# A decoder trunk on one core: the last LayerNorm's reciprocal root rewritten with one step on GpSimd, and the 16 spatial products of the gMLP mixer dealt out differently

## Chip, core and metric

The kernel is one program on one core of a Trainium2 chip. The metric is the device time of one execution in microseconds (us). Engines are named as in the profile: PE (TensorE, matmuls; PEld is its weight load), DVE (VectorE), ACT (ScalarE), POOL (GpSimd), SP (SyncE, which here only starts DMAs).

## What is computed

Two post-norm layers over x (1 x 1024 x 1024). Layer 0 mixes tokens with a gated MLP (gMLP), layer 1 with dilated attention; each mixer is followed by a squared-ReLU MLP. After each of the four sub-layers the residual is normalized. Cut to what the change touches:

```python
def layer_norm(x, g, b):
    mu = jnp.mean(xf, axis=-1, keepdims=True)
    var = jnp.mean(jnp.square(xf - mu), axis=-1, keepdims=True)
    y = (xf - mu) * lax.rsqrt(var + LN_EPS) * g + b

def mixer_a(h, w_in, b_in, vn_g, vn_b, w_s, b_s, w_out):
    u, v = jnp.split(jax.nn.gelu(h @ w_in + b_in), 2, axis=-1)
    v = layer_norm(v, vn_g, vn_b).reshape(B, S // CHUNK, CHUNK, A_GROUPS, A_GROUP_DIM)
    z = jnp.einsum('gts,bnsgc->bntgc', w_causal, v) + b_s.T[:, :, None]
    return (u * z.reshape(B, S, A_WIDTH)) @ w_out

for i in range(DEPTH):                      # DEPTH = 2
    x = layer_norm(ALPHA * x + gate * mixer(h), ln_g[i, 0], ln_b[i, 0])
    x = layer_norm(ALPHA * x + gate * squared_relu_mlp(h), ln_g[i, 1], ln_b[i, 1])
```

## The kernel before

The program runs five stages one after another: the gMLP mixer (to about 306 us), the first MLP, the attention, its output product, and the second MLP, whose end is the end of the program. Every product is done in three passes of 128x512 matmuls on pairs (hi, lo) of rounded numbers; making the pair from a raw tile takes a cast (usually on ACT, L107) and a subtraction (usually on DVE, L108), the helper `split`. Instructions are recorded in the order of the code; the Tile layer then orders each engine's queue, and each engine runs its queue in order.

**The mixer.** v stands in the tile `vz` (8 row blocks of 128 tokens by 1024 columns), in two halves of 512 columns. `norm_v(ch, i)` normalizes half `ch` of row block `i`: one ACT step (L583) and two DVE steps (L584, L585). `spatial(g)` does the product of group g, 64 columns of all eight row blocks: the pair `vhi`, `vlo` (two buffers each, so group g+2 takes over those of group g), three matmuls into the bank `psz` (L377), and on ACT the result back into `vz` (L595). Groups 0 to 7 read the first half of the columns, groups 8 to 15 the second, so `norm_v(1, ...)` of all eight row blocks must be done before group 8. `u_unit(u)` makes 128 columns of u (48 matmuls into `psu`), `gate_unit(u)` transposes groups 2u and 2u+1 (`pszt`, L615) and multiplies them with u (L616). A loop over u deals the groups out between the units:

```python
for u in range(KD):
    for _ in range((2, 2, 2, 3, 3, 4, 0, 0)[u]):
        g = groups_of.popleft()
        spatial(g)
        if g < NT:
            norm_v(1, g)
```

Meanwhile a background queue (`tick`) works through the adaLN products: it loads `adaw` tiles, adds them up on DVE in `adaacc` (L133), and sums over partitions with the small matmuls `psa` (L167, L168; L159 and L160 for a gate). The output weights `wout` and the last `winu` tiles are loaded and split in the same stretch.

**The second MLP's end.** Its down product goes through seven passes of eight steps, each with its own pair of splits, prepared two steps ahead (`rhi`, `lhi` on ACT, `rlo`, `llo` on DVE, L972 on PE). The last three steps are done row block by row block for m = 0 to 3, 18 matmuls each, and each row block then ends so: add the product to the residual (L992), statistics (L256), mean and variance (L321 into `mv`), `rstd_of` (L244 variance plus epsilon; L245 square root on ACT; L246 reciprocal r; L248 r*r*(var+eps); L252 times -0.5 plus 1.5; L253 times r), then the result in two steps over 1024 columns (L341: (z - mean) * g; L342: times rstd, plus b) and the DMA out. The row of g (`lng`) is loaded by `affine`, in the middle of the down product. Row blocks 4 to 7 end earlier, between other steps.

Of the kernel before, what the change touches and what calls it, by code (L numbers as in the profile page):

```python
# [10 lines left out]
F32 = mybir.dt.float32  # L11
F32R = mybir.dt.float32r
AF = mybir.ActivationFunctionType
ALU = mybir.AluOpType
# [3 lines left out]
P = 128  # L18
S = 1024
D = 1024  # L20
NT = S // P
# [8 lines left out]
EPS = 1e-5  # L30
# [5 lines left out]
def trunk(ctx: ExitStack, tc: tile.TileContext, x, c, ada_w, ada_b, ln_g, ln_b, a_w_in, a_b_in,  # L36
# [4 lines left out]
    V, A, G, T = nc.vector, nc.scalar, nc.gpsimd, nc.tensor  # L41

    def pool(stack, name, bufs, **kw):
        return stack.enter_context(tc.tile_pool(name=name, bufs=bufs, reuse_waits="tile", **kw))

    cst = pool(ctx, "cst", 1)
    small = pool(ctx, "small", 4)
# [10 lines left out]
    ident = cst.tile([P, P], F32, name="ident")  # L58
    make_identity(nc, ident[:])
    ones_r = cst.tile([P, P], F32R, name="ones_r")  # L60

    n_ln = 4 * KD
    o_g, o_b, o_s, o_i = 0, n_ln, 2 * n_ln, 2 * n_ln + 16
# [177 lines left out]
    def rstd_of(dst, var, n, name):  # L241

        t = small.tile([P, 3, n], F32, name=name, tag=f"rstd{n}", bufs=4 if n == 1 else 1)
        V.tensor_scalar(t[:, 0, :], var, EPS, None, ALU.add)  # L244
        A.activation(t[:, 1, :], t[:, 0, :], AF.Sqrt)  # L245
        V.reciprocal(t[:, 2, :], t[:, 1, :])  # L246
        if n == 1:
            V.scalar_tensor_tensor(t[:, 1, :], t[:, 2, :], t[:, 2, :], t[:, 0, :], ALU.mult, ALU.mult)  # L248
        else:
            V.tensor_tensor(t[:, 1, :], t[:, 2, :], t[:, 2, :], op=ALU.mult)  # L250
            V.tensor_tensor(t[:, 1, :], t[:, 1, :], t[:, 0, :], op=ALU.mult)
        V.tensor_scalar(t[:, 1, :], t[:, 1, :], -0.5, 1.5, ALU.mult, ALU.add)  # L252
        V.tensor_tensor(dst, t[:, 1, :], t[:, 2, :], op=ALU.mult)  # L253
# [9 lines left out]
    def row_tile(src, name, tag):  # L263
        t = vec.tile([P, D], F32, name=name, tag=tag)
        nc.sync.dma_start(t[:], src.partition_broadcast(P))
        return t
# [3 lines left out]
    class Residual:  # L270
# [19 lines left out]
        def affine(self, j):  # L290
            i, s = divmod(j, 2)
            self.g = row_tile(ln_g[i, s], f"lng_{j}", "lng")
            self.b = row_tile(ln_b[i, s], f"lnb_{j}", "lnb")

        def add_x(self, i):
            j = self.j
            t = work.tile([P, D], F32, name=f"res_{j}_{i}", tag="res", bufs=3)
            nc.sync.dma_start(t[:], (spill[j - 1] if j else x_in)[i * P : (i + 1) * P, :])
            V.scalar_tensor_tensor(self.acc[i][:], t[:], ALPHA, self.acc[i][:], ALU.mult, ALU.add)
# [18 lines left out]
        def moments(self, i):  # L318

            mv = self.mv[i] = small.tile([P, 4], F32, name=f"mv_{self.j}_{i}", tag="mv")  # L320
            V.bn_aggr(mv[:, 0:2], self.st.pop(i)[:])  # L321
            rstd_of(mv[:, 2:3], mv[:, 1:2], 1, f"r_{self.j}_{i}")

        def finish(self, i, halves=(0, 1)):
            j = self.j
# [132 lines left out]
    def mixer_a():  # L458
        nonlocal ada_p, vec
        with ExitStack() as ph:  # L460
# [88 lines left out]
            with tc.tile_pool(name="mixA1", bufs=3, reuse_waits="tile") as a1:  # L549
# [22 lines left out]
                mv = ap.tile([P, 4, NT], F32, name="mv_v")  # L572
# [7 lines left out]
                def norm_v(ch, i):  # L580
                    w = slice(ch * HALF, (ch + 1) * HALF)
                    z = vz[:, i, w]
                    A.activation(z, z, AF.Identity, bias=mv[:, 3, i : i + 1], scale=mv[:, 2, i : i + 1])  # L583
                    V.tensor_tensor(z, z, vg[:, w], op=ALU.mult)  # L584
                    V.tensor_tensor(z, z, vb[:, w], op=ALU.add)  # L585

                def spatial(g):
                    w = slice(g * HEAD, (g + 1) * HEAD)
                    hi = a1.tile([P, NT, HEAD], F32R, name=f"vhi_{g}", tag="vhi", bufs=2)
                    lo = a1.tile([P, NT, HEAD], F32R, name=f"vlo_{g}", tag="vlo", bufs=2)  # L590
                    split(hi[:], lo[:], vz[:, :, w])
                    p = bank("mm", f"psz_{g}")
                    p3 = p[:].rearrange("p (n c) -> p n c", c=HEAD)
                    passes(p3, [([t[:, g, :] for t in wsT], [hi[:], lo[:]])])
                    A.activation(vz[:, :, w], p3, AF.Identity, bias=cols[:, o_s + g : o_s + g + 1])  # L595
# [26 lines left out]
                uts = [u_unit(0), u_unit(1)]  # L622
                groups_of = deque(range(16))
                for u in range(KD):
                    for _ in range((2, 2, 2, 3, 3, 4, 0, 0)[u]):
                        g = groups_of.popleft()
                        spatial(g)
                        if g < NT:
                            norm_v(1, g)
                    if u + 2 < KD:  # L630
                        uts.append(u_unit(u + 2))
                    gate_unit(u, uts[u])
# [1209 lines left out]
    with ExitStack() as ph:  # L1842
        open_psum(ph, "A", tr=3, mm=5)
        done = mixer_a()
# [33 lines left out]
```

## Time and profile before

| | us |
|---|---|
| three runs | 2695.23, 2697.97 (median), 2700.25 |
| the profiled execution's own time | 2695.87 |
| its span, first to last instruction | 2694.1 |
| PE busy in the span | 2650.0 |
| DVE busy in the span | 1992.2 |
| ACT busy in the span | 1375.9 |
| POOL busy in the span | 116.5 |

The span is 1.8 us shorter than the execution's own time; the predicted times are times of the execution. A row of the timeline gives the start (us from the first instruction), the length, the engine, the line, the operation and its tiles, and in brackets how long the engine had been idle before and what released it. A row of the waits gives the total, the number and the longest. Matmuls are pipelined: the next one starts about 0.23 us after the last, though each is listed with 0.39 us.

### The profile page before, as it was taken

To read this page: it belongs to the slowest core of one execution; us is meant where nothing else is said; L and a number is where in the kernel's file an instruction comes from. 1 tells how busy PE (TensorE), PEld (TensorE's weight loads), DVE (VectorE), ACT (ScalarE), POOL (GpSimd) and SP (SyncE) were. 2 spreads that over 40 slices of the span, in tenths; PEclk is the share of its full clock that TensorE was granted. 3 is DMA by queue.
4 is the path that set the end of the run, shared out by engine and by line. 5 is a ranking of instruction groups with operands and counts; after the bars stand their busy time and mean duration, and the time that the engine had idled before them with its cause. 6 is when DMAs were issued, how large, how long until landed. Compare 5 with 4: busy or idle time off the path is not lost.

```text
span 2694.1 us, 37100 instructions
## 1 busy us (share of the span) xinstructions
PE 2650.0 (98%) x13242; PEld 2190.0 (81%) x13242; DVE 1992.2 (74%) x3610; ACT 1375.9 (51%) x2601; POOL 116.5 (4%) x193
## 2 busy tenths in 40 slices
PE   6999999999999999999999999999999999999998
PEld 5787878888888888888888888888888788888887
DVE  6687698787888788655647777777658966577877
ACT  3354375555544464333436666666655655553332
POOL 1000000000000001111111000000010000000000
PEclk9999999999999999999999999999999999999999
DMA  8444337676967745655476545555683664485562
GB/s 266 149 129 130 125 122 230 221 240 232 360 225 251 243 157 192 208 182 191 165 224 176 138 127 139 140 145 145 206 233 122 200 206 154 148 308 196 179 209 82
DMA packets 340781, 504.77 MB, mean 187 GB/s; under 512 B 51900, under 2 KB 177252, under 8 KB 340596
## 3 DMA queue, kind: packets, MB, share of 16 engines
q1 hardware_dynamic: 324212, 443.68, 51.9%
q0 software_dynamic: 16384, 58.73, 6.0%
q8 instruction: 104, 1.70, 0.3%
q14 instruction: 81, 0.66, 0.1%
HBM read 365.40 MB, written 136.92 MB: 186 GB/s over the span
## 4 chain that ended last, share of the span: by engine, by line
PE 56%; issue 22%; DVE 9%; DMA 8%; POOL 2%; ACT 2%; SPq 0%; POOLq 0%; DVEq 0%; ACTq 0%
PE psd L972 11%; PE psua L810 8%; PE psk L1402 6%; PE psq L1402 6%; DMA adaw<-in_ada_w_dram 4%; PE psuc L810 4%; PE psd_wout L398 3%; PE pv L1571 3%; PE sc L1491 3%; PE psu L377 2%; PE psub L810 2%; PE psv L480 2%; DVE adaacc L133 1%; PE pT L1544 1%; POOL v L1278 1%
## 5 line engine op out<-in xcount | busy, mean ns | idle before, releaser
L810 PE MATMUL psua<-right,left 128*128 128x512 f32 x1536 | 364.8, 391 | 0.5 <-ACT part L815 0.2
L972 PE MATMUL psd<-rhi,lhi 128*128 128x512 f32 x896 | 349.7, 390 | 0.0
L972 PE MATMUL psd<-rlo,lhi 128*128 128x512 f32 x896 | 348.8, 389 | 0.0
L972 PE MATMUL psd<-rhi,llo 128*128 128x512 f32 x896 | 348.6, 389 | 0.0
L810 PEld LDWEIGHTS psua<-right,left 128*128 128x128 f32 x1536 | 286.4, 188 | 63.8 <-ACT part L815 1.6
L1513 ACT ACTIVATE p<-p,stat 128x128 f32<-128x128 f32 (+1 forms) x384 | 168.8, 441 | 98.1 <-DVE stat L1511 97.9
L972 PEld LDWEIGHTS psd<-rhi,lhi 128*128 128x128 f32 x896 | 168.2, 188 | 35.8 <-ACT part L841 0.9
L972 PEld LDWEIGHTS psd<-rhi,llo 128*128 128x128 f32 x896 | 168.3, 188 | 35.1
L972 PEld LDWEIGHTS psd<-rlo,lhi 128*128 128x128 f32 x896 | 168.3, 188 | 34.4
L810 PE MATMUL psuc<-right,left 128*128 128x512 f32 x768 | 188.6, 392 | 0.1
L133 DVE SCALAR_TENSOR_TENSOR adaacc<-adaw,silu_c,adaacc 128x512 f32<-128x512 f32 x168 | 128.5, 775 | 59.4 <-DMA adaw<-in_ada_w_dram 58.5
L810 PEld LDWEIGHTS psuc<-right,left 128*128 128x128 f32 x768 | 143.0, 188 | 31.9 <-DVE right L108 1.2
L108 DVE TENSOR_TENSOR pTlo<-pT,pThi 128x512 fp32r<-128x512 f32 (+1 forms) x160 | 99.3, 621 | 75.6 <-ACT pThi L107 74.6
L107 ACT CAST left<-ws 128x512 fp32r<-128x512 f32 x128 | 79.4, 621 | 140.5 <-DVE ws L730 103.6
L108 DVE TENSOR_TENSOR llo<-lraw,lhi 128x1024 fp32r<-128x1024 f32 x112 | 136.3, 1218 | 2.3 <-ACT lhi L107 2.3
L108 DVE TENSOR_TENSOR left<-ws,left 128x512 fp32r<-128x512 f32 x128 | 88.0, 689 | 66.2 <-ACT left L107 63.9
L1402 PE MATMUL psk<-form_L,wqk_hi 128*128 128x512 f32 x384 | 127.1, 412 | 0.2 <-DVE qlo L108 0.2
L1402 PE MATMUL psq<-form_L,wqk_hi 128*128 128x512 f32 x384 | 126.4, 410 | 0.0
L107 ACT CAST lhi<-lraw 128x1024 fp32r<-128x1024 f32 x112 | 117.1, 1047 | 7.1 <-PE psd L972 3.3
L1301 PE MATMUL psv<-vrhi,form_S 128*128 128x512 f32 x384 | 119.9, 390 | 0.8 <-ACT vrhi L107 0.5
L1511 DVE CUSTOM_DVE_ANT_0 p<-sc,bias 128x128 f32<-128x128 f32 (+1 forms) x384 | 113.9, 346 | 5.6 <-PE sc L1491 4.6
L107 ACT CAST pThi<-pT 128x512 fp32r<-128x512 f32 (+1 forms) x160 | 84.7, 530 | 59.3 <-PE pT L1544 42.6
(332 smaller groups left out, 6070.9 us busy)
## 6 DMA issues: line engine op xcount, KB each, us to landing
lraw<-forms SPq DMA_DIRECT2D x112, 512.0 KB, 3.6
adaw<-in_ada_w_dram SPq DMA_DIRECT2D x192, 256.0 KB, 3.0
up<-in_mlp_w_up_dram SPq DMA_DIRECT2D x64, 512.0 KB, 4.4
forms<-s SPq DMA_DIRECT2D x128, 256.0 KB, 3.0
rraw<-in_mlp_w_down_dram SPq DMA_DIRECT2D x64, 512.0 KB, 5.4
forms<-part SPq DMA_DIRECT2D x96, 256.0 KB, 2.4
v<-vs POOLq DMA_DIRECT2D x48, 512.0 KB, 3.7
vraw<-in_b_w_qkv_dram SPq DMA_DIRECT2D x42, 512.0 KB, 3.9
```

The source lines that it names most:

```text
L107: first = A.copy(hi, src) if hi_engine is A else hi_engine.tensor_copy(hi, src)
L108: return first, lo_engine.tensor_tensor(lo, src, hi, op=ALU.subtract)
L133: ins = V.scalar_tensor_tensor(acc[:], raw[:], silu_c[:, k : k + 1], acc[:], ALU.mult, ALU.add)
L398: T.matmul(p[:], stat[a][:, k, o : o + P], u[b][:, w], start=n == 0, stop=n == count - 1)
L810: T.matmul(acc, w[:, a, k, :], right[p][:, b, k, :], start=p in (1, 2, 5) and k + a + b == 0, stop=k == 3 and a == 1, skip_group_check=True)
L972: ins = T.matmul(sums[kind, m][:], l[a][:, k, m * P : (m + 1) * P], r[b][:, k, :], start=p in (1, 5, 2, 3) and kp + k + a + b == 0, stop=k ...
L1301: T.matmul(acc, rows[:, m * P : (m + 1) * P], cols_, start=p in (1, 2, 5) and kp + k + a + b == 0, stop=kp == 1 and k == 1 and a == 1, ski ...
L1402: T.matmul(p[:], wu[a][:, k * P : (k + 1) * P], h_op(k, half, b), start=k + c_ == 0, stop=k == KD - 1 and c_ == 2)
L1491: T.matmul(banks[e][:, sl], q_[a][rows, tq], k_[b][rows, keys], start=c_ == 0, stop=c_ == 2)
L1511: V.tensor_tensor_reduce(out=pr, in0=banks[e][:, sl], in1=st["bias"][:, width - w :], scale=-0.125, scalar=3e38, op0=ALU.add, op1=ALU.min, ...
L1513: A.activation(pr, pr, AF.Exp, bias=nm, scale=-1.0, accum_out=l)
L1571: T.matmul(pvs[b][:, q0 % HALF : q0 % HALF + w_], stt, x_[:, o_ : o_ + w_], start=not begun[b], stop=left[b] == 0, skip_group_check=True)
```

## The change

Three edits, in four places.

1. In the last LayerNorm alone (j = 3) the correction of the root goes from three DVE steps to two. With s = r*r*(var+eps), r*(1.5 - 0.5*s) is -0.5 * (s - 3) * r; the kernel now leaves rstd without the -0.5, and the row of g is multiplied by -0.5 once, on ACT, behind its load. Variance plus epsilon for s is made on GpSimd instead of DVE, beside the square root, which adds epsilon itself from a new constant tile `eps`.
2. That constant is set by DVE at the start of the program. The tile lies ahead of nearly all others: in the built program 3068 SBUF tiles lie 32 bytes further, 343 lie where they lay.
3. The groups are dealt out as 2, 2, 3, 3, 3, 3 instead of 2, 2, 2, 3, 3, 4, and `norm_v(1, ...)` of the eight row blocks is spread over groups 0 to 5 instead of 0 to 7.

```diff
+    eps = cst.tile([P, 1], F32, name="eps")
+    V.memset(eps[:], EPS)
...
             self.b = row_tile(ln_b[i, s], f"lnb_{j}", "lnb")
+            if j == 3:
+                A.mul(self.g[:], self.g[:], -0.5)
...
             V.bn_aggr(mv[:, 0:2], self.st.pop(i)[:])
-            rstd_of(mv[:, 2:3], mv[:, 1:2], 1, f"r_{self.j}_{i}")
+            if self.j < 3:
+                rstd_of(mv[:, 2:3], mv[:, 1:2], 1, f"r_{self.j}_{i}")
+                return
+            t = small.tile([P, 3, 1], F32, name=f"r_{self.j}_{i}", tag="rstd1", bufs=4)
+            G.tensor_scalar(t[:, 0, :], mv[:, 1:2], EPS, None, ALU.add)
+            A.activation(t[:, 1, :], mv[:, 1:2], AF.Sqrt, bias=eps[:])
+            V.reciprocal(t[:, 2, :], t[:, 1, :])
+            V.scalar_tensor_tensor(t[:, 1, :], t[:, 2, :], t[:, 2, :], t[:, 0, :], ALU.mult, ALU.mult)
+            V.scalar_tensor_tensor(mv[:, 2:3], t[:, 1, :], -3.0, t[:, 2, :], ALU.add, ALU.mult)
...
-                    for _ in range((2, 2, 2, 3, 3, 4, 0, 0)[u]):
+                    for _ in range((2, 2, 3, 3, 3, 3, 0, 0)[u]):
                         g = groups_of.popleft()
                         spatial(g)
-                        if g < NT:
-                            norm_v(1, g)
+                        for i in ((0, 1), (2,), (3,), (4,), (5, 6), (7,))[g] if g < 6 else ():
+                            norm_v(1, i)
```

In the changed file the lines stand 2 lower from the constant on, 4 lower behind `affine` and 12 lower behind `moments`. Where the change moves rows, on three engines:

PE, in the mixer, where group 8 is multiplied (names as in the text above; the first number in a name is the group or the unit). Before:

```order
L377 MATMUL psz_7_1819<-vhi_7_1815,wsT_0_777 128x512
L377 MATMUL psz_7_1819<-vlo_7_1816,wsT_0_777 128x512
L377 MATMUL psz_7_1819<-vhi_7_1815,wsT_1_778 128x512
L167 MATMUL psa_1_0_1_1912<-ones_r_78,adahi_1_0_1_1898 128x2
L377 MATMUL psz_8_1831<-vhi_8_1827,wsT_0_777 128x512
L377 MATMUL psu_5_0_1843<-hT_0_0_0_129,winu_5_hi_1838 128x512
L377 MATMUL psu_5_0_1843<-hT_0_0_1_130,winu_5_hi_1838 128x512
L377 MATMUL psu_5_0_1843<-hT_0_0_0_129,winu_5_lo_1839 128x512
L377 MATMUL psz_8_1831<-vlo_8_1828,wsT_0_777 128x512
```

In the change group 8 stands second behind group 7, and the third of its cluster, group 9, comes behind eight `psa` and five transposes; these are the last rows of that stretch:

```order
L170 MATMUL psa_1_0_1_1923<-ones_r_78,adalo_1_0_1_1910 128x2
L627 MATMUL pszt_3_0_1942<-ident_73,vz_129 128x128 x4
L627 MATMUL pszt_3_1_1948<-ident_73,vz_129 128x128
L389 MATMUL psz_9_1842<-vhi_9_1838,wsT_0_779 128x512
L389 MATMUL psu_5_0_1854<-hT_0_0_0_131,winu_5_hi_1849 128x512
L389 MATMUL psu_5_0_1854<-hT_0_0_1_132,winu_5_hi_1849 128x512
L389 MATMUL psu_5_0_1854<-hT_0_0_0_131,winu_5_lo_1850 128x512
L389 MATMUL psu_5_0_1854<-hT_0_0_0_131,winu_5_hi_1849 128x512
L389 MATMUL psz_9_1842<-vlo_9_1839,wsT_0_779 128x512
```

So the third group of a cluster has more other work ahead of it than before. PE at the last groups, 14 and 15 before:

```order
L159 MATMUL psa_1_2_0_2165<-adahi_1_2_0_2043,ones_r_78 128x512
L160 MATMUL psa_1_2_0_2165<-adalo_1_2_0_2044,ones_r_78 128x512
L615 MATMUL pszt_5_0_2183<-ident_73,vz_127 128x128 x4
L615 MATMUL pszt_5_1_2189<-ident_73,vz_127 128x128 x4
L377 MATMUL psz_14_2086<-vhi_14_2082,wsT_0_777 128x512
L377 MATMUL psz_15_2095<-vhi_15_2091,wsT_0_777 128x512
L377 MATMUL psu_7_0_2107<-hT_0_0_0_129,winu_7_hi_2102 128x512
L377 MATMUL psz_14_2086<-vlo_14_2083,wsT_0_777 128x512
```

and now, with group 14 done in one piece and 15 transposes ahead of group 15:

```order
L389 MATMUL psz_14_2088<-vhi_14_2084,wsT_0_779 128x512
L389 MATMUL psz_14_2088<-vlo_14_2085,wsT_0_779 128x512
L389 MATMUL psz_14_2088<-vhi_14_2084,wsT_1_780 128x512
L627 MATMUL pszt_5_0_2185<-ident_73,vz_129 128x128 x4
L627 MATMUL pszt_5_1_2191<-ident_73,vz_129 128x128 x4
L627 MATMUL pszt_6_0_2197<-ident_73,vz_129 128x128 x4
L627 MATMUL pszt_6_1_2203<-ident_73,vz_129 128x128 x3
L389 MATMUL psz_15_2097<-vhi_15_2093,wsT_0_779 128x512
L389 MATMUL psu_7_0_2109<-hT_0_0_0_131,winu_7_hi_2104 128x512
```

The transposes of unit 6 used to stand behind the whole of `psu_7`; most of them now stand ahead of group 15. DVE at the end of the program, from the last row block's statistics on (`mv_3`, `r_3` and `xo` 24702 are the last row block's, `mv_2` and `xo` 24669 the one's before it), before:

```order
L256 BN_STATS st_3_24572<-acc_3_22393 128x6
L252 TENSOR_SCALAR r_2_24662<-r_2_24662 128x1
L321 BN_AGGR mv_3_24693<-st_3_24572 128x2
L253 TENSOR_TENSOR mv_2_24660<-r_2_24662 128x1
L244 TENSOR_SCALAR r_3_24695<-mv_3_24693 128x1
L341 SCALAR_TENSOR_TENSOR xo_24702<-acc_3_22393,mv_3_24693,lng_23717 128x512
L342 SCALAR_TENSOR_TENSOR xo_24669<-xo_24669,mv_2_24660,lnb_23719 128x1024
L246 RECIPROCAL r_3_24695<-r_3_24695 128x1
L341 SCALAR_TENSOR_TENSOR xo_24702<-acc_3_22393,mv_3_24693,lng_23717 128x512
L248 SCALAR_TENSOR_TENSOR r_3_24695<-r_3_24695 128x1
L252 TENSOR_SCALAR r_3_24695<-r_3_24695 128x1
L253 TENSOR_TENSOR mv_3_24693<-r_3_24695 128x1
```

and now:

```order
L334 SCALAR_TENSOR_TENSOR mv_2_24657<-r_2_24659 128x1
L258 BN_STATS st_3_24571<-acc_3_22395 128x6
L354 SCALAR_TENSOR_TENSOR xo_24665<-xo_24665,mv_2_24657,lnb_23721 128x1024
L325 BN_AGGR mv_3_24689<-st_3_24571 128x2
L353 SCALAR_TENSOR_TENSOR xo_24697<-acc_3_22395,mv_3_24689,lng_23719 128x512
L332 RECIPROCAL r_3_24691<-r_3_24691 128x1
L353 SCALAR_TENSOR_TENSOR xo_24697<-acc_3_22395,mv_3_24689,lng_23719 128x512
L333 SCALAR_TENSOR_TENSOR r_3_24691<-r_3_24691 128x1
L334 SCALAR_TENSOR_TENSOR mv_3_24689<-r_3_24691 128x1
```

Two small rows of each row block are gone, and the second result step of the row block before stands ahead of the last one's L325 instead of behind its first L353. On ACT, in the middle of the second MLP's down product (pass 6 is the third), the scaling of g stands between two casts:

```order
L109 CAST lhi_5_7_22971<-lraw_5_7_22931 128x1024
L109 CAST rhi_5_7_22976<-heldt_1_22412 128x1024
L109 CAST lhi_6_0_23010<-lraw_6_0_22968 128x1024
L297 ACTIVATE lng_23719<-lng_23719 128x1024
L109 CAST rhi_6_0_23015<-heldt_0_22411 128x1024
```

Before, the two casts of step 6_0 stood one behind the other.

## The prediction

> **What bounds the kernel now.** I read the page's first part, then the waits of PE, then the timeline at the places that the change touches.
>
> ```profile
> span 2694.1 us, 37100 instructions
> PE 2650.0 (98%) x13242; PEld 2190.0 (81%) x13242; DVE 1992.2 (74%) x3610; ACT 1375.9 (51%) x2601; POOL 116.5 (4%) x193
> ```
>
> PE idles 44.1 us of 2694.1, so work that lies beside PE is worth nothing by itself; an edit pays where PE waits or after PE's last matmul.
>
> ```profile
> PE psa L167 <- ACT adahi L107: 16.8, 3, 13.9
> ...
> PE psz L377 <- DVE vlo L108: 0.7, 1, 0.7
> PE psz L377 <- ACT vhi L107: 0.7, 1, 0.7
> ```
>
> Of the waits that the list names, the mixer's spatial products hold only 1.4 us. The longest, 13.9, is at the start, where the first adaLN sum is formed. The end is DVE's: PE's last matmul starts at 2683.81, and DVE works in one piece from row block 0 to the last result step.
>
> ```profile
> 2683.58 0.39 PE L972 MATMUL psd<-rlo,lhi 128*128 128x512 f32 x1
> 2683.81 0.39 PE L972 MATMUL psd<-rhi,llo 128*128 128x512 f32 x1
> ```
>
> **Part 1, the groups.** The timeline of the first wait, PE and ACT:
>
> ```profile
> 210.81 0.16 PE L167 MATMUL psa<-ones_r,adahi 128*128 128x2 f32 x1
> ...
> 211.62 1.09 PE L615 MATMUL pszt<-ident,vz 128*128 128x128 f32 x8
> 212.47 0.47 PE L377 MATMUL psz<-vhi,wsT 128*128 128x512 f32 x1
> ...
> 213.01 0.63 PE L377 MATMUL psz<-vhi,wsT 128*128 128x512 f32 x2
> ...
> 213.71 0.39 PE L377 MATMUL psz<-vhi,wsT 128*128 128x512 f32 x1
> ...
> 214.75 0.50 PE L377 MATMUL psz<-vhi,wsT 128*128 128x512 f32 x1 [0.65 <-ACT vhi L107]
> ...
> 247.25 0.50 PE L377 MATMUL psz<-vlo,wsT 128*128 128x512 f32 x1 [0.69 <-DVE vlo L108]
> ```
>
> ```profile
> 213.50 0.69 ACT L595 ACTIVATE vz<-psz,cols 128x512 f32<-128x512 f32 x1 [0.58 <-PE psz L377]
> 214.09 0.61 ACT L107 CAST vhi<-vz 128x512 fp32r<-128x512 f32 x1
> ```
>
> Group 8 is third behind 6 and 7 and takes over group 6's `vhi`. Group 6's last matmul starts at 213.01, ACT writes its result back from 213.50, casts until 214.70, and PE starts group 8 at 214.75: 1.74 us that PE must fill between the first product's last matmul and the third product. Before, it had that matmul's own step, group 7 (together 0.93, to 213.94) and one `psa`, and stood 0.65.
>
> In the new order every cluster but the first two has three groups, with this ahead of the third. Eight `psa` take 0.81 (210.81 to 211.62), eight transposes 0.85 (211.62 to 212.47). Group 6: 0.93 plus eight `psa`, 1.74: just covered. Group 9: 0.93 plus 0.81 plus five transposes (0.53), 2.27. Group 12: 0.93 plus eight transposes (0.85) plus two `psa` of 512 columns at about 0.23, 2.24. Group 15: 0.93 plus 15 transposes (1.6), 2.5. All reach 1.74, so both waits should go: 1.34 us. New ones are possible. Fifteen transposes for units 5 and 6 need banks that DVE must empty, and DVE may be in a 128x1024 subtraction for `wout` (such a step takes 1.22 us by L1722's row in part 2); and the `vlo` behind a `vhi` has just three `psu` matmuls (0.7) to hide its 0.69. I charge 0.35 for both, nearer to the single waits shown than to the 1.22. Term: **-1.0 us**, between -1.3 and +0.9 (both waits kept in a new place, plus 0.9).
>
> What moves with it: the second half's norms come up to three groups earlier, two DVE steps and one ACT step each. They pass background additions and `winu` splits, all needed a unit later (48 matmuls 0.23 us apart, 11 us), and DVE's longest waits between 150 and 330 us are for its loads:
>
> ```profile
> DVE adaacc L133 <- DMA adaw<-in_ada_w_dram: 11.4, 13, 2.0
> ```
>
> The DMAs of `winu_7`, `wout_0`, `wout_2` and `wout_3` move by one to three places on SP, far ahead of use. I price these at nothing; without that cover a late weight would cost PE a whole split, 1 to 2 us.
>
> **Part 2, the last rows.** DVE at row block 0:
>
> ```profile
> 2673.45 0.21 DVE L321 BATCH_NORM_AGGREGATE mv<-st 128x2 f32<-128x12 f32 x1
> 2673.69 0.15 DVE L244 TENSOR_SCALAR r<-mv 128x1 f32<-128x1 f32 x1
> 2673.76 1.27 DVE L341 SCALAR_TENSOR_TENSOR xo<-acc,mv,lng 128x1024 f32<-128x1024 f32 x1
> 2674.95 0.15 DVE L246 RECIPROCAL r<-r 128x1 f32<-128x1 f32 x1
> 2675.14 0.22 DVE L248 SCALAR_TENSOR_TENSOR r<-r 128x1 f32<-128x1 f32 x1
> 2675.40 0.15 DVE L252 TENSOR_SCALAR r<-r 128x1 f32<-128x1 f32 x1
> 2675.59 0.16 DVE L253 TENSOR_TENSOR mv<-r 128x1 f32<-128x1 f32 x1
> 2675.78 1.28 DVE L342 SCALAR_TENSOR_TENSOR xo<-xo,mv,lnb 128x1024 f32<-128x1024 f32 x1
> ...
> 2684.54 0.67 DVE L992 TENSOR_TENSOR acc<-acc,psd 128x512 f32<-128x512 f32 x1
> ...
> 2689.50 1.42 DVE L342 SCALAR_TENSOR_TENSOR xo<-xo,mv,lnb 128x512 f32<-128x512 f32 x2
> ```
>
> Read by starts. Without L244 the next step waits for L321 itself (0.24) instead of for L244: 0.07 gained. Of L248, L252, L253 and the step to L342 (0.26, 0.19, 0.19) one 0.19 goes. So 0.26 a row block, 1.04 for four, but not all reaches the end: the last row block's L992 starts at 2684.54, only 0.34 behind the end of PE's last matmul (2683.81 plus 0.39), and the new order puts the block before's 1.2 us result step ahead of its L325 without dropping anything else. Its own 0.26 stays, and of the others at most 0.34: **-0.3 us**, between -0.6 and 0 by this alone.
>
> The add on POOL must not come late. POOL and DVE side by side, in attention:
>
> ```profile
> L1479 POOL TENSOR_SCALAR bias<-near x32: 397/408/1451, 1418.3 to 1966.6; 128x256 f32<-128x256 f32 x32
> ```
>
> ```profile
> 1418.22 1.22 DVE L1722 TENSOR_TENSOR aff<-aff,aff_g 128x1024 f32<-128x1024 f32 x1
> 1419.47 1.30 DVE L1722 TENSOR_TENSOR aff<-aff,aff_b 128x1024 f32<-128x1024 f32 x1
> ```
>
> The same POOL step takes 408 ns, but 1451 when it starts at 1418.3 beside a wide DVE step of two SBUF tiles: it ends at 1419.7, 0.27 behind that step, and the next one takes 1.30 in place of 1.22. In the new tail L353 is such a step, and starts as the add does. If the add ends 0.27 behind L353, r's correction (L333, 0.19 behind L332) comes about 0.1 to 0.2 late; the add is one column, not 256, so I take 0 and keep 0.2 for each of four row blocks, 0.8, in the range. [...]
>
> **Part 3, g times -0.5.** It costs ACT one step and makes the casts behind it wait for the load of g.
>
> ```profile
> L306 ACT ACTIVATE lng<-lng x2: 1061/1061/1061, 689.8 to 2394.2; 128x1024 f32<-128x1024 f32 x2
> ...
> heldr<-in_mlp_w_down_dram SPq DMA_DIRECT2D x16, 512.0 KB, 7.5
> ```
>
> ```profile
> 2453.85 0.34 SPq L265 DMA_DIRECT2D lng<-in_ln_g_dram  x1
> ```
>
> ```profile
> 2455.56 1.05 ACT L107 CAST rhi<-heldt 128x1024 fp32r<-128x1024 f32 x1 [3.44 <-PE psd L972]
> ...
> 2464.57 1.95 ACT L986 COPY dpart<-psd 128x512 f32<-128x512 f32 x3 [1.57 <-PE psd L972]
> ```
>
> The cast at 2455.56 is `rhi` of step 6_0; PE reaches that step when pass 5 is evicted, at 2464.57. g's load starts at 2453.85. With the slowest median of a 512 KB load, 7.5, the scaling ends at 2462.4, the cast at 2463.5 and `rlo` at 2464.7, late by 0.1; any shorter load leaves it early. Cost 0, at most 0.5; ACT idles 3.44 us each step and recovers.
>
> **Part 4, the constant and the shift.** DVE's memset at the start is one more like those of 0.17 us; soon after, DVE waits for a load anyway:
>
> ```profile
> 7.99 0.75 DVE L133 SCALAR_TENSOR_TENSOR adaacc<-adaw,silu_c,adaacc 128x512 f32<-128x512 f32 x1 [0.69 <-DMA adaw<-in_ada_w_dram]
> ```
>
> So it is hidden; uncovered it costs 0.2. The 32 bytes touch nearly every operand. Some tiles lay 96 bytes off a multiple of 128 before (`acc`, the `adaw` of all but the first stage, `khi`), most at 0; all of the latter go to 32.
>
> ```profile
> L130 DVE TENSOR_SCALAR adaacc<-adaw,silu_c x24: 479/486/2578, 5.8 to 2144.8; 128x512 f32<-128x512 f32 x24
> ```
>
> ```profile
> L1544 PE MATMUL pT<-ident,p 128*128 128x128 f32 x384 | 81.9, 272 | 0.0
> ...
> L712 PE MATMUL pst<-ident,acc 128*128 128x128 f32 x128 | 19.7, 275 | 1.0 <-ACT acc L261 0.9
> ```
>
> The L130 group reads both kinds and has one length, 479 to 486; PE transposes `acc` (off) in 275 ns and `p` (even) in 272. Price 0. [...]
>
> **Sum.** -1.0 - 0.3 = -1.3 us against the execution's 2695.87, so 2694.6. The median of the three runs is 2.1 above that execution; against it the forecast is 2697.97 - 1.3 = **2696.7**. A difference under about 0.2% (5.4 us) cannot be told from no change here.
>
> **Rivals.**
> - *Nothing is gained*: POOL's add takes the tail's gain back (0.8 against 0.3) and new waits for `vlo` or the transposes' banks take the place of the mixer's 1.34. Sum between -0.3 and +1.4, about +0.5: 2698.5. For: POOL's 1451. Against: the fillers counted above. 25%.
> - *Slower by the shift* (the other side): an operand 32 bytes off costs each 128x512 matmul a little. The mechanism has a place, the streams of PE, which fill 98% of the span, and decides from 0.46 ns a matmul: at 0.23 us a step (2683.58 to 2683.81) about 11700 make the span, so 0.46 ns each is 5.4 us, and 2 ns is 23 us, 2720. Against: the 275 to 272 above, 3 ns at most, and on a transpose. For: no wide matmul in the page streams an offset tile except a few gate sums. 8%. [...]
> - *The mixer gains more*: gaps too short for the list of waits may go too; were each of 16 products shortened by 0.3, that is 5 us: 2691.7. Against: in the worst 20 us of that stretch PE is busy for 19.19 of 20, by the row behind this list. 7%.
>
> ```profile
> 240.00:260.00 20.00, 19.19 (x93) 15.28 (x92) 15.31 (x23) 10.54 (x18) 0.00 (x0) 1.00 0.37 106
> ```
>
> **How the numbers follow.** The forecast has 55%. Own scatter of the runs is -2.7 to +2.3 about the median; with the bounds of the sum (-1.9 to +2.4 with all costs) the range is **2691.0 to 2702.7**, which takes in the first rival and the third and leaves out the shift on PE. Faster by over 0.2% needs less than 2692.6: the third rival and a lucky draw, 10%. Slower needs over 2703.4: the shift and an unlucky draw, 10%. Between: 80%.
>
> **What would show it.** PE's waits for `vhi` and `vlo` in the mixer gone, 240 to 260 us without idle time; unit 6's transposes not named as waiting for DVE. From the last L992 to the last result steps 4.6 us in place of 4.96 (2684.54 to 2689.50), the add on POOL ending before L332 has ended. `rhi` of step 6_0 shifted by 2 to 7 us with PE unmoved. Matmuls 0.23 us apart as before. Wrong, if PE's step in the long passes has grown, or if PE waits longer than 13.9 us for the first sum.

## The result, and the profile after

The change is slower: 2706.37 us (median of 6 runs, 2700.58 to 2707.66) against 2697.02 us for the kernel before (6 runs, 2695.23 to 2703.70), ratio 1.0028, 95% interval 1.0016 to 1.0040. The prediction was 2696.7, with 2702.7 as its upper end. Three executions in a slow state are left out of all comparisons: one of e6 (12233 us) and two of the kernel before (3711 beside e9 to e12, 3297 beside g1 and g2). The profile of the change, its first lines:

```profile
span 2705.4 us, 37108 instructions
...
PE 2654.0 (98%) x13242; PEld 2193.2 (81%) x13242; DVE 1990.6 (74%) x3595; ACT 1377.6 (51%) x2602; POOL 123.4 (5%) x201
```

The span has grown by 11.3 us and PE's busy time by 4.0, so 7 us are new idle time of PE, and 4 us are matmuls that took longer. The waits of PE (total, number, longest):

```profile
PE psa L169 <- ACT adahi L109: 15.8, 3, 13.6
...
PE sc L1503 <- DMA bk<-qk: 4.5, 2, 4.3
...
PE psua L822 <- ACT part L827: 1.4, 2, 1.1
...
PE psz L389 <- ACT vhi L109: 0.7, 1, 0.7
```

The first wait is as before (13.9). The mixer's wait for `vlo` is gone, the one for `vhi` is still there. The new one, 4.3 us for `bk`, is in the attention, 1.7 ms behind the last row that the new order moves in the mixer. It stood at 0.38 before. The timeline of PE there, before and after:

```profile
1982.97 0.98 PE L1491 MATMUL sc<-bk,bq 64*128 64x256 f32 x12 [0.38 <-DMA bk<-qk]
```

```profile
1991.39 1.65 PE L1503 MATMUL sc<-bk,bq 64*128 64x256 f32 x12 [4.32 <-DMA bk<-qk]
1992.97 0.79 PE L1787 MATMUL psob<-wo_hi,oTs 128*128 128x512 f32 x1
1993.56 0.63 PE L1787 MATMUL psob<-wo_lo,oTs 128*128 128x512 f32 x1
```

Behind the wait the same twelve matmuls take 1.65 us in place of 0.98. The view of stretches of the change shows why (PE busy comes first behind the length; the granted clock is the third number from the end):

```profile
1987.00:1991.00 4.00, 0.08 (x1) 0.00 (x0) 0.56 (x1) 1.36 (x5) 0.86 (x1) 1.00 0.70 199
1991.00:1996.00 5.00, 4.61 (x20) 3.83 (x21) 1.47 (x8) 1.16 (x5) 0.00 (x0) 0.50 0.85 175
1996.00:2000.00 4.00, 4.00 (x20) 3.41 (x20) 0.97 (x2) 3.06 (x8) 0.29 (x1) 0.77 0.15 49
```

Behind the pause the granted clock was 0.50 over the 5 us of the second stretch and 0.77 over the 4 us of the third; in finer stretches it was 0.50 from 1991.0 to 1997.5, 0.68 over the half us behind and 1.00 from 1998.0, together some 6.8 us at 0.50. Most of the 4 us of longer matmuls are here: the stretch around the wait ("bk" in the table below) has grown by 6.8 us, the wait itself by 3.9, so 2.9 are longer matmuls. SP's queue tells why `bk` is late; first before, then after:

```profile
1970.52 0.37 SPq L1626 DMA_DIRECT2D mst<-st_dram  x1
1970.98 0.45 SPq L1441 DMA_DIRECT2D v<-v  x1
1971.53 0.54 SPq L1606 DMA_DIRECT2D st_dram<-stat  x1
1977.97 0.36 SPq L1626 DMA_DIRECT2D mst<-st_dram  x1
...
1979.04 0.60 SPq L1459 DMA_DIRECT2D bk<-qk  x1
```

```profile
1975.88 0.37 SPq L1638 DMA_DIRECT2D mst<-st_dram  x1
1976.35 1.54 SPq L1453 DMA_DIRECT2D v<-v  x1
1977.98 0.53 SPq L1618 DMA_DIRECT2D st_dram<-stat  x1
1986.24 0.36 SPq L1638 DMA_DIRECT2D mst<-st_dram  x1
...
1987.31 0.60 SPq L1471 DMA_DIRECT2D bk<-qk  x1
```

SP issues `mst`, which reads back statistics just written to DRAM, only when that write has landed: 6.4 us later before, 8.3 after. The loads of `bk` stand behind it in the same queue. This is one half of the delay. The other is that the write itself (`st_dram`) was issued later, 5.3 us behind the start of PE's 10001st matmul in place of 3.3: it stands behind an earlier `mst` in the queue, which waits in the same way, and behind a load of `v`, whose issue took 1.54 us in place of 0.45.

To see where the rest went, I took the start times of PE's 13242 matmuls and compared stretches between the same matmuls (us; "start" ends at the 420th, "mixer" is 800th to 1090th, "MLP 1" 2000th to 2800th, "bk" 10085th to 10120th, "end" runs from the last matmul's start to the end of the span). The kernels of the later rows are the experiments below:

```
                        start    mixer    MLP 1     bk      end
before                  113.20   61.81    178.35    6.05    10.33
after                   116.09   60.78    179.37   12.87    10.33
e5 (after, again)       115.48   62.78    182.68    9.19    10.33
e1 (edits, no shift)    116.39   61.00    180.55    6.51    10.31
e2 (32 bytes alone)     114.67   61.69    177.49    6.94    10.34
e3 (groups alone)       114.23   61.54    179.37   12.00    10.32
e9 (groups, again)      115.55   60.95    178.89    6.78    10.32
e4 (LayerNorm alone)    112.88   61.16    177.05    6.15    10.31
f1 (before, mst moved)  114.26   61.27    178.77    5.61    10.32
f2 (after, mst moved)   113.88   62.83    181.14    5.60    10.33
g2 (e1, mst moved)      113.41   60.62    181.13    5.61    10.31
```

Single executions scatter by 1 to 2 us in "start" and "MLP 1", and by 6 in "bk". The end has not moved at all, and the mixer not for sure. So the profiles alone don't say which edit did it.

### The profile page after: what moved, and what is told of

Read it like the earlier page. It is cut to its first block, busy times and chain, and to the rows that moved or that the text cites. A ratio compares the mean times of both kernels' runs of the same rounds, so it can differ in the third digit from the quotient of the medians.

```text
span 2705.4 us, 37108 instructions
## 1 busy us (share of the span) xinstructions
PE 2654.0 (98%) x13242; PEld 2193.2 (81%) x13242; DVE 1990.6 (74%) x3595; ACT 1377.6 (51%) x2602; POOL 123.4 (5%) x201
## 4 chain that ended last, share of the span: by engine, by line
PE 53%; issue 22%; DVE 10%; DMA 9%; ACT 3%; POOL 2%; SPq 0%; POOLq 0%; DVEq 0%; ACTq 0%
PE psd L984 11%; PE psua L822 7%; PE psk L1414 6%; PE psq L1414 5%; DMA adaw<-in_ada_w_dram 4%; PE psuc L822 3%; PE psd_wout L410 3%; PE psu L389 3%; PE pv L1583 3%; PE sc L1503 3%; PE psub L822 2%; DVE adaacc L135 2%; PE psv L492 1%; PE pT L1556 1%; DVE left L110 1%
```

## The experiments

Theory S: the 32 bytes by which the constant moves nearly every tile make the loss. Rivals: G, the new order of the groups, and L, the last LayerNorm's edit. In the results, "mean difference" is that of the kernel's runs to the runs of the kernel before made beside it (10 to 12 runs, 4 or 5 of e11, e12 and f4, against 20 to 35).

**The parts apart: e1 to e4.** The kernel before allocates a tile of 96 bytes named `pad` in `small` that nothing uses; with it `act`, the pool behind, starts on a multiple of 256 bytes. e1 is the change with its constant put there, so that no tile moves:

```diff
-    small.tile([P, 24], F32, name="pad", bufs=1)
+    pad = small.tile([P, 24], F32, name="pad", bufs=1)
...
-    eps = cst.tile([P, 1], F32, name="eps")
-    V.memset(eps[:], EPS)
+    eps = pad[:, 0:1]
+    V.memset(eps, EPS)
```

> All edits of the change, but the constant for epsilon is one column of the 96-byte tile named pad that the kernel before allocates and does not use, so that all 3411 tiles of the kernel before keep their places. Theory S (the 32 bytes alone make the loss of 1.0028): the loss is gone and the sum of the prediction is left, -0.5 to -2 us against the kernel before, ratio 0.9993 to 0.9999; DMA packets of 512 bytes in the first 100 us are back at a mean of 27.6 ns (30.4 in the change) and no wait of PE for bk is near 4.3 us. Theory G (the new order of the groups moves weight loads and the norms, and this throws the later stages out of step): still 1.0028, since the order is unchanged. Theory L (the last LayerNorm's edit: the memset at the start, the scaling of g, GpSimd's add, eight more instructions): still 1.0028.

Measured: 1.0005 (0.9996 to 1.0013), mean difference +1.9. As S expects, the packets of 512 bytes are back at 27.7 ns, and the longest wait for `bk` is 0.84 us; the gain that S left to the edits is not seen. e2 is the kernel before with the shift and nothing else:

```diff
     ones_r = cst.tile([P, P], F32R, name="ones_r")
+    cst.tile([P, 1], F32, name="gap")
```

> The kernel before with nothing but a tile of 128x1 behind ones_r that nothing writes or reads: the instructions and their order are those before, and 3068 tiles lie 32 bytes further, as in the change. Theory S: slower by the change's loss plus the 1 to 1.5 us that its edits gain, ratio 1.0028 to 1.0040 (7 to 11 us), with the start's psws and adaw waits longer by 2 to 3 us and the bk wait of about 4 us at 1985 to 1995 us. Theories G and L: 1.000, within 2 us.

Measured: 1.0015 (1.0004 to 1.0026), mean difference +4.8, and runs up to 2711.2 where none of 35 runs of the kernel before was above 2704.5. That is less than the 7 to 11 us that S expected, and the profiled execution, the fastest of the 12, waits 1.26 us for `bk`, not 4. e3 has only the new dealing of groups and norms (third edit of the diff), e4 only the LayerNorm's edit, its constant in `pad`.

> The kernel before with the new dealing of the groups and norms alone; no tile moves. Theory S: the mixer's -1.2 us that the trace of the change shows between its starts of 200 and 261 us, ratio 0.9993 to 1.0000. Theory G: the whole loss, 1.0025 to 1.0035. Theory L: 1.000.

> The kernel before with the edit of the last LayerNorm alone, the constant in the unused pad tile, so that no tile moves. Theory S: -0.3 us, ratio 0.9996 to 1.0002. Theory G: 1.000. Theory L: the whole loss, 1.0025 to 1.0035.

Measured: e3 1.0003 (0.9992 to 1.0013), e4 0.9994 (0.9985 to 1.0002). So of the three parts an unused tile of 32 bytes is the only one that is slower beyond its interval. L falls. G is not excluded by e3's interval, and e3's profiled execution has waits like those of the change:

```profile
PE sc L1491 <- DMA bk<-qk: 3.8, 1, 3.8
...
PE psua L810 <- ACT part L815: 1.2, 1, 1.2
```

**e9** therefore ran e3's kernel once more.

> The kernel before with the new dealing of the groups alone, once more, since e3's interval (0.9992 to 1.0013) holds both answers. Theory A: the new order is worth nothing, in the mixer or behind it, and e3's long waits behind it (1.2 us for psua at 629 us, 3.8 us for bk at 1988 us) are draws that every kernel has: 0.9995 to 1.0005, the trace's stretch from PE's 800th to its 1090th matmul at 61 to 62 us (61.81 before). Theory G: its order of loads makes the later waits likelier: 1.0006 to 1.0015, with the waits for psua and bk together over 2 us again.

Measured: 1.0001 (0.9991 to 1.0011), and its `bk` stretch was 6.78. The long wait for `bk` is a draw that an unshifted kernel has too: e3 had it, e9, the same program, had not. G as the cause of the whole loss falls.

**How far, and where to: e5 to e8.** e5 is the change again; e6, e7 and e8 are e2 with 64, 128 and 256 bytes.

```diff
+    cst.tile([P, 16], F32, name="gap")     e6; P, 32 in e7; P, 64 in e8
```

> The change itself once more, on the chip of the three shifts below. If the first comparison holds (1.0028), it comes out at 1.0020 to 1.0036. Theory S2 (the 32 bytes give 1.0015 as e2 measured, the rest comes from the new order of the groups, as e1 over e4 suggests: 1.0005 against 0.9994): 1.0015 to 1.0030, and its trace shows waits of PE for psua's eviction near 630 us and for bk near 1990 us. Theory N (most of the first difference was scatter: this kernel's runs spread over 10 us): 1.0000 to 1.0012.

> The kernel before with an unused tile of 128x16 behind ones_r: 3068 tiles lie 64 bytes further. Theory B64 (a DMA write that does not start on 64 bytes is slower): packets of 512 bytes back at a mean of 27.5 ns as in the kernel before, time 0.9995 to 1.0005. Theory B256 (the start has to lie on 256 bytes): packets as slow as with 32 bytes, 30 ns or more, time 1.0010 to 1.0025. Theory of any move: 1.0010 to 1.0025 with packets unchanged.

> The same with a tile of 128x32: 128 bytes further. Theory B64: 27.5 ns and 0.9995 to 1.0005. Theory B256: 30 ns or more and 1.0010 to 1.0025. Theory of any move: 1.0010 to 1.0025 with packets unchanged.

> The same with a tile of 128x64: 256 bytes further; by B64 and B256 alike 27.5 ns and 0.9995 to 1.0005. Only the theory that any move of the tiles costs expects 1.0010 to 1.0025.

Measured: e5 1.0014 (1.0005 to 1.0023), mean difference +4.6 (the first comparison's was +7.6, from six runs each). That is under the 1.0020 that was expected if the first comparison held; a part of the first difference may have been scatter. The shifts, with what the first 100 us of the DMA records hold, which start some 11 us ahead of the first instruction (mean length of the 6312 packets of 512 bytes; share of the 2048-byte packets that took exactly 84 ns):

```
shift         512 bytes    2048 at 84 ns    ratio to before
0 (before)    27.6 ns          86%          1
32   e2       30.2             66           1.0015 (1.0004 to 1.0026)
64   e6       29.9             68           1.0012 (1.0004 to 1.0021)
128  e7       29.3             85           1.0005 (0.9996 to 1.0013)
256  e8       27.4             89           1.0005 (0.9996 to 1.0013)
change        30.4             63           1.0028, 1.0014
```

The packets of 512 bytes are a clean answer: they are back at the old length only with 256. Those of 2048 bytes are not: fewer take exactly 84 ns, but their mean is 94 to 97 ns in every row. Around the wait for `bk` it is otherwise. In the 32 us from 20 us ahead of PE's 10001st matmul, the 2304 packets of 2048 bytes took 87.5 to 87.8 ns on average in the five traces with 32 or 64 bytes, f2 below among them, 86.9 with 128, and 84.8 to 85.2 in the eleven where no tile or `raw` alone is moved off 256. The times go the same way as the packets, but 128 and 256 bytes differ from 32 by no more than their intervals. In these loads the tile that moved is the one written; why packets take longer there is not shown.

**Which wait: f1, f2.** One word moves the wait for the statistics out of SP's queue, in the kernel before (f1) and in the change (f2):

```diff
-                        nc.sync.dma_start(st[:, g].rearrange("p s (e n) -> p (s e) n", n=NT),
+                        nc.gpsimd.dma_start(st[:, g].rearrange("p s (e n) -> p (s e) n", n=NT),
```

> The kernel before with one word changed: the loads mst, which wait for the statistics' way through DRAM (st_dram), are issued by GpSimd's queue instead of SP's, so that SP does not stand in front of the loads of bk and bq until they are due. Theory H (every kernel here stands at PE's wait for bk near 1985 us in some runs, 0.4 us in the profiled run before and 4 to 6 us in others, since SP waits there for st_dram): the wait is gone, the stretch between PE's 10085th and 10120th matmul is 6.0 us in every run, and the time is 0.9988 to 0.9998. If this wait is rare: 1.000. If GpSimd's queue answers too slowly: slower, with PE or DVE waiting for mst.

> The change with the same word changed. If the 32 bytes make their loss by way of the wait for bk: 0.9995 to 1.0005 against the kernel before, 3 to 5 us under the change. If they make it elsewhere (the loads of the first 110 us and of the first MLP): 1.0010 to 1.0020, no more than 1 us more gained than in f1.

Measured: f1 0.9995 (0.9986 to 1.0004), mean difference -1.4; f2 1.0006 (0.9997 to 1.0015), +1.1, which lies between its two answers. The timeline of f1, SP's queue and PE's scores:

```profile
1967.92 1.00 SPq L1606 DMA_DIRECT2D st_dram<-stat  x1
1974.48 0.57 SPq L1459 DMA_DIRECT2D bq<-qk  x1
1975.14 0.56 SPq L1459 DMA_DIRECT2D bk<-qk  x1
```

```profile
1980.29 0.97 PE L1491 MATMUL sc<-bk,bq 64*128 64x256 f32 x12
1983.57 0.98 PE L1491 MATMUL sc<-bk,bq 64*128 64x256 f32 x12
```

`bk` is issued some 4 us earlier, and PE's rows have no wait in brackets any more. The scatter of the runs fell with it: the standard deviation of f1's 11 runs is 1.0 us, that of the 27 runs of the kernel before beside them 2.4 (highest 2699.2 and 2704.6). In the other kernels with `mst` moved it fell less: 1.5 in f2, 1.5 and 1.8 in g1 and g2 below, beside which the kernel before had 1.8. So this wait makes a part of the scatter, and how large a part is not settled. It costs the kernel before 1.4 us on average (standard error 0.5), and the change 3.5 (4.6 less 1.1, by e5) to 6.5 (by the first comparison). So 2 to 5 us of the change's loss come by way of this wait, the 2 with a standard error of 1.2. With the wait out of the way f2 is still 2.5 us above f1 (standard error 0.5).

What the shift does to this wait is seen in SP's queue. With `mst` on SP, the four traces with 32 or 64 bytes issue the write `st_dram` 3.8 to 5.3 us behind the start of PE's 10001st matmul (4.6 on average), and the nine without (those with operands moved apart left out) 2.9 to 3.8 (3.3). From there to `mst` it is 6.9 us on average in the four and 7.2 in the nine. So it is not the write that is longer with the shift: the queue comes to it later. With `mst` moved it is issued 1.3 us ahead of that matmul.

**The rest: g1, g2.** g2 is e1 with f1's word: the edits without shift and without that wait. g1 is f1 with 224 unused bytes at the upper end, which puts the later `adaw` tiles on multiples of 256; e10 is those bytes alone:

```diff
     act = pool(ctx, "act", 4)
+    pool(ctx, "gap", 1, side="right").tile([P, 56], F32, name="gap")
```

> All edits of the change with no tile moved (e1), and mst on GpSimd's queue (f1): with f1 and f2 it separates the edits from the 32 bytes where the wait for bk is out of the way. If the edits gain nothing (mixer and tail both 0 in the traces) and the 32 bytes make f2's distance from f1: as f1, 2696.8 to 2698.5 us beside f1's 2697.7, and 2 us under f2. If the edits cost something of their own (more waits for psua in the first MLP): as f2, 1.0003 to 1.0008. If they gain what was forecast: 0.9990 or less.

> The kernel before with 224 unused bytes at the upper end: adaw of the later stages, acc and the attention's qhi, qlo, khi, klo, which lie 224 bytes behind a multiple of 256 before, come to lie on one; nothing else moves. If a DMA packet's start on 256 bytes is what counts (e2, e6 to e8), the 160 adaw loads land sooner (median now 3.0 us, then 2.8 to 2.95) and their waits in the first MLP shrink: 0.9988 to 1.0000. If the loss of e2 comes from what the engines read, or from the loads of one stage alone, 1.000 and an unchanged landing time.

> f1 together with the 224 unused bytes of e10, which put the later adaw tiles, acc and the attention's q and k pairs on multiples of 256. In f1 the scatter of the runs fell from 2.3 to 0.9 us, so a difference of 1 us can now be seen. If landing on 256 bytes shortens the waits for adaw in the first MLP: 0.5 to 2 us under f1, 0.9985 to 0.9993 against the kernel before. If not: as f1, 0.9993 to 0.9997.

Measured: g2 1.0000 (0.9991 to 1.0009), mean difference -0.5; e10 0.9995 (0.9986 to 1.0004); g1 0.9993 (0.9984 to 1.0002), -1.9. g2 lies between f1 (-1.4) and f2 (+1.1), by 0.9 and 1.6 us with standard errors of 0.9, so the other 2.5 us of f2 can't be divided between the shift and the edits. e10's landing time of `adaw` is the old one, 3.0 us; that alignment gains there is not shown. g1 is the lowest of all, but its interval still holds the kernel before.

**Where the landing is: f3, e11, e12, f4.** f3 puts only the two buffers `raw` 32 bytes off, which DMAs fill and no matmul reads:

```diff
-            raw = wts.tile([P, D], F32, name=f"{name}_raw", tag="raw", bufs=2)[:]
+            raw = wts.tile([P, D + 32], F32, name=f"{name}_raw", tag="raw", bufs=2)[:, 8 : D + 8]
...
```

> The kernel before with only the two buffers raw 32 and 160 bytes behind a multiple of 256 (each tile is 128 bytes wider and used from its ninth column on); they take the raw weights of the mixer and of q and k, and two of five loads of the MLPs, and no matmul reads them. All above lies 256 bytes further, so PE's operands keep their distance. If slower DMA packets alone make the loss: 512-byte packets at about 30 ns in the first 100 us, time 1.0004 to 1.0012, PE's matmuls 227 ns apart as before. If the loss of e2 needs the engines' operands off: 1.000.

Measured: 0.9999 (0.9990 to 1.0008), with 512-byte packets at 29.8 ns. So slow packets into these buffers cost at most some 2 us, and nothing that is seen here; most of e2's loss is with other tiles. e11 and e12 were to split the rest by pools, `act` off and all else on 256, or the reverse:

```diff
+    pool(ctx, "gap", 1).tile([P, 8], F32, name="gap")       e11; in e12 behind act
     act = pool(ctx, "act", 4)
+    pool(ctx, "gap2", 1).tile([P, 56], F32, name="gap2")    e11 only
```

> The kernel before with only the four 16 KB tiles of the pool act 32 bytes off (hT, right, heldt, heldr, oTs, the forms); all that lies above them lies 256 bytes further, so its starts on 256 bytes are kept. If the weight loads (winv, winu, up, rraw, lraw, ws) carry the loss: 1.0000 to 1.0006. If oTs and the forms, which hold up the loads of bk, carry it: 1.0012 to 1.0020.

> The complement: act stays, what lies above it is 32 bytes off. If the weight loads carry the loss: 1.0010 to 1.0020, with 512-byte packets at about 30 ns in the first 100 us. If oTs and the forms carry it: 1.0000 to 1.0006.

Measured: 1.0076 (1.0061 to 1.0091) and 1.0081 (1.0065 to 1.0098). Both expectations missed by 15 us and more, and both kernels by the same, so they don't answer their question. They answer another. Groups of e2, where both operands of `psua` lie 32 bytes further, and of e12, where only `left` does:

```profile
L811 PE MATMUL psua<-right,left 128*128 128x512 f32 x1536 | 364.5, 391 | 0.7 <-ACT part L816 0.4 <-ACT right L108 0.2
L973 PE MATMUL psd<-rhi,lhi 128*128 128x512 f32 x896 | 349.7, 390 | 0.0
```

```profile
L811 PE MATMUL psua<-right,left 128*128 128x512 f32 x1536 | 371.6, 395 | 0.3 <-ACT right L108 0.2
L973 PE MATMUL psd<-rhi,lhi 128*128 128x512 f32 x896 | 349.7, 390 | 0.0
```

`psua` has grown, `psd`, whose operands moved together, has not. From start to start (median) `psua`'s matmuls are 227 ns apart in the kernel before, in e2 and in the change, 233 in e11 and 232 in e12. So for `psua` it is the distance of the two operands that counts: 32 bytes between them cost 5 to 6 ns a matmul. f4 is e12 with 64:

> e12 with 64 bytes in place of 32: act stays, all above it lies 64 bytes further. e11 and e12 made psua's matmuls 233 ns apart in place of 227, and only where the two operands of a matmul lie 32 bytes apart in their place within 64 bytes (rhi and lhi, moved together, kept 227). Theory R64: a distance of 64 costs PE nothing, 227 ns, time 1.0000 to 1.0012. Theory R256: any distance that is no multiple of 256 costs the same 6 ns, 1.0070 to 1.0090.

Measured: 1.0076 (1.0062 to 1.0089), 233 ns: a distance of 64 costs the same.

## Why the prediction was wrong

**The step that failed is part 4's "Price 0"** for the shift. It cost 4.8 us (e2, standard error 1.5). The step looked at PE and DVE reading tiles off and on, found no difference, and that much held: the change's psua matmuls are 227 ns apart, as before. But the same tiles are filled by DMAs, and packets did get slower: those of 512 bytes at the start (27.6 to 30.2 ns), those of 2048 bytes around the wait for `bk` (85 to 87.5). That they are what makes the queue late is argued from the times, not shown by a run of its own. The loads ahead of the first sum show no loss: the wait there was 13.6 in place of 13.9. PE hides slower loads into `raw` (f3, within 2 us), but not one chain, the write and read-back of the statistics with `bk` queued behind them, through which 2 to 5 us went (f1, f2); the rest of the loss has no place yet. Before, PE was 0.38 us short of hiding that chain, and the row was in the trace. It was not quoted, because it was small. A wait of 0.4 us at the end of a chain of DMAs in one execution is a sign that there is no slack, not that the cost is 0.4. Neither of the two signs of being wrong that the prediction named came: `psua` kept its step, and the first wait was not longer than 13.9.

**The rival "slower by the shift"** had the sign and the cause, and the wrong place: PE's streams, with 8%. e11, e12 and f4 show that this mechanism exists (5 to 6 ns a matmul, over the 0.46 from which the rival lets it decide) but not in this change, which moves both operands alike (227 ns, as before).

**Part 1, -1.0.** Both waits that were to go went, and a new one came: group 6, "just covered". PE and ACT in the change:

```profile
201.82 0.63 PE L389 MATMUL psz<-vhi,wsT 128*128 128x512 f32 x2
...
202.51 0.39 PE L389 MATMUL psz<-vhi,wsT 128*128 128x512 f32 x1
...
203.44 0.25 PE L170 MATMUL psa<-ones_r,adalo 128*128 128x2 f32 x1
204.36 0.50 PE L389 MATMUL psz<-vhi,wsT 128*128 128x512 f32 x1 [0.67 <-ACT vhi L109]
```

```profile
202.16 1.05 ACT L109 CAST winu_hi<-winu_raw 128x1024 fp32r<-128x1024 f32 x1 [0.80 <-DMA winu_raw<-in_a_w_in_dram]
203.12 0.68 ACT L607 ACTIVATE vz<-psz,cols 128x512 f32<-128x512 f32 x1
203.70 0.61 ACT L109 CAST vhi<-vz 128x512 fp32r<-128x512 f32 x1
```

The eight `psa` are there. But ACT has a weight cast of 1.05 us in its queue ahead of the copy back, so from the first product's last matmul (201.82) to the third product it is 2.54 us in place of the 1.74 that the prediction wanted covered. All seven traces with the new order have this wait, of 0.50 to 1.21 us. In two of them the granted clock was 0.50 for 3.4 us right behind it, in e5 from 204.7 (the 128x512 matmuls start 0.43 us apart there and 0.23 later) and in f2 from 203.2 us; the row of the wait in e5:

```profile
204.09 0.50 PE L389 MATMUL psz<-vhi,wsT 128*128 128x512 f32 x1 [1.15 <-ACT vhi L109]
```

The mixer's stretch is 62.8 us in these two and 61.0 on average in the other five, so the new order gained some 0.5 where the clock held, and lost 1.3 where it did not. Over all traces it is 61.5 us in the seven with the new order and 61.5 in the ten with the old one (those with operands moved apart left out): the term was 0.

**Part 2, -0.3.** The end took 10.33 us from PE's last matmul, as before. DVE in the change:

```profile
2695.72 0.16 DVE L332 RECIPROCAL r<-r 128x1 f32<-128x1 f32 x1
2695.99 0.22 DVE L333 SCALAR_TENSOR_TENSOR r<-r 128x1 f32<-128x1 f32 x1
2696.12 0.68 DVE L1004 TENSOR_TENSOR acc<-acc,psd 128x512 f32<-128x512 f32 x1
...
2700.71 1.42 DVE L354 SCALAR_TENSOR_TENSOR xo<-xo,mv,lnb 128x512 f32<-128x512 f32 x2
```

From the last L1004 to the last result steps it is 4.59 us, as forecast (4.6). But L333 of the row block before now stands ahead of L1004 and waits for its reciprocal, where the kernel before had L992 right behind L246. L1004 starts 1.08 us behind the start of PE's last matmul (2695.04), in place of 0.73; the 0.35 are given back at once. POOL's add was about as long as the L353 that started just ahead of it on DVE, as that rival said: 1.23 us with 1.28 over 1024 columns, 0.70 with 0.75 over 512:

```profile
2694.64 1.23 POOL L330 TENSOR_SCALAR r<-mv 128x1 f32<-128x1 f32 x1 [3.57 <-DVE mv L325]
2698.99 0.70 POOL L330 TENSOR_SCALAR r<-mv 128x1 f32<-128x1 f32 x1 [3.12 <-DVE mv L325]
```

It ends at 2695.87, just as the reciprocal does (2695.88). L333 starts 0.27 us behind L332, where the prediction had 0.19, so the add costs at most 0.08 here.

**Part 3, 0**, was right. The load of g, issued at 2464.62, had landed 3.7 us later, within the 7.5 allowed for. The cast behind it came 2.5 us late against the end of pass 5 (at 2475.80 here, 2464.57 before), within the 2 to 7 that were named, and without moving PE: its last 1741 matmuls span 394.95 us in both kernels.

```profile
2468.32 1.06 ACT L297 ACTIVATE lng<-lng 128x1024 f32<-128x1024 f32 x1 [4.98 <-DMA lng<-in_ln_g_dram]
2469.29 1.04 ACT L109 CAST rhi<-heldt 128x1024 fp32r<-128x1024 f32 x1
```

**The sum.** With no tile moved the edits give 1.0005 (e1) and 1.0000 (g2) in place of 0.9995; the traces put both terms at 0. The base of the sum was not at fault: the forecast stood on 2697.97 for the kernel before, and 2697.02 was measured beside the change.

**What stays open.** How the 32 bytes' loss divides beyond the wait for `bk`: "start" is 115.3 us on average in the five traces with 32 or 64 bytes and 114.4 in the twelve others, within the scatter. And MLP 1: 180.5 us on average in the seven traces with the new order of groups, 178.6 in the ten with the old one, though nothing there has been reordered and e3 and e9 are no slower than the kernel before by their times. PE's waits there are for ACT's copy of `part`, which stands behind a cast that waits for `adaw`; why the new order should lengthen them was not tried. That a shifted kernel meets the long wait for `bk` more often is concluded from the times of e2, e5, f1 and f2 and from the later issue of `st_dram`; of the traces themselves two of four with 32 or 64 bytes have it and two of nine without (`mst` on SP), too few to show it. Whether the longer packets ahead of `st_dram` make its issue late was not tried.

## What to carry to other kernels

A new small tile ahead of everything is an edit to every address behind it: look whether the bulk tiles keep their starts on 256 bytes, and put small constants into padding that is already there (32 bytes more cost 4.8 us here, e2, and made the 512-byte packets 30.2 ns; with the constant in `pad`, e1, they took 27.7). When loads get a little slower, look for the one chain of dependent DMAs that the engine barely hides, here a read-back in SP's queue with urgent loads behind it (a wait of 0.38 us before, 4.32 in the change), and take the read-back out of that queue (worth 1.4 us here, within the interval of the ratio). In an engine's order, what stands directly ahead of the last step counts as much as how many steps there are (here 0.35 us lost against 0.37 gained).

## What the runs showed of the hardware

- In the first 100 us, DMA packets of 512 bytes took 27.6 ns on average where tiles start on a multiple of 256 bytes (the kernel before), 30.2, 29.9 and 29.3 with 32, 64 and 128 bytes more (e2, e6, e7), and 27.4 with 256 (e8). Packets of 2048 bytes took 85 ns around the wait for `bk`, and 87.5 with 32 or 64 bytes more.
- A pause of PE can cost more than its length. With waits for `bk` of 0.38 to 1.26 us the `bk` stretch was 6.0 to 6.9 us; with 2.00 (e5), 3.36 (e10), 3.76 (e3) and 4.32 (the change) it was 9.2, 11.5, 12.0 and 12.9, that is 1.6 to 2.9 more than the wait itself over f1's 5.6, with a granted clock of 0.50 for some 6.8 us behind the longest. The length of the wait did not decide it alone: in the mixer the clock was 0.50 behind waits of 1.15 (e5) and 1.21 us (f2), and behind e2's 1.26 for `bk` it was 1.00, with the twelve matmuls at 0.98 us. What decides it is not shown. e5's twelve matmuls took 1.24 us, in place of 0.98, behind 2.00 (the profile names `pTlo` for this wait; it is counted as one for `bk` because in the kernel before the same `sc` ran ahead of that row, and because it starts 4.0 us behind the issue of `bk`, before 3.9):

```profile
1992.72 1.24 PE L1503 MATMUL sc<-bk,bq 64*128 64x256 f32 x12 [2.00 <-DVE pTlo L110]
1993.89 0.79 PE L1787 MATMUL psob<-wo_hi,oTs 128*128 128x512 f32 x1
1994.48 0.63 PE L1787 MATMUL psob<-wo_lo,oTs 128*128 128x512 f32 x1
```

- Two operands of a matmul whose places differ by 32 or 64 bytes from a multiple of 256 made the 128x512 matmuls of `psua` 232 to 233 ns apart in place of 227, and the kernel 0.8% longer (e11, e12, f4); with both moved together they stayed 227 apart (e2).
